# Sparse attention scores on TensorE: the low-part product widened from 64 to 128 stationary rows

## The chip, the cores and the metric

The kernel runs on one core of a Trainium2 chip. The metric is the device time of one execution in microseconds (us). Three executions of the kernel before took 1151.09, 1152.84 and 1153.11 us; the median is 1152.84 us.

## What is computed

Two layers over 256 tokens of 1024 features. Each layer is half a SwiGLU block, a token mixer, and half a SwiGLU block, each followed by a residual, a layer norm and a modulation. The mixer of layer 0 is retention, that of layer 1 sparse attention with 16 heads in 4 groups. With 256 tokens all four key blocks are selected and the window holds all keys, so two of its three branches are dense causal attentions over 256 keys, each with keys and values of its own:

```python
q = q.reshape(B, S, G, HPG, dh) * (dh ** -0.5)          # G 4, HPG 4, dh 64
s = jnp.einsum('qghd,gqnkd->ghqnk', qi, k_g) - slopes * dist_s      # branch "selected"
...
s = jnp.einsum('qghd,kgd->ghqk', qi, kwb) - slopes * dist_w         # branch "window"
p = masked_softmax(s, mask_w, -1)
...
o = gb[..., 0:1] * o_cmp + gb[..., 1:2] * o_sel + gb[..., 2:3] * o_win
```

The change touches the two einsums for `s`: a product of queries and keys over dh = 64.

## The kernel before

Every fp32 value that enters a product is split exactly into a high and a low float32r part, and a product is the sum of high by high, high by low and low by high. Weights stream in as chunks of [128, 2048] (1 MB), are split into `wh` and `wl` by ScalarE, VectorE and GpSimd, and are used by TensorE in the order of a written plan.

Sparse attention is stage 4 of 6. Its work is a hand-written list of step names, `NSA_STEPS`, which `Program.run` calls one after the other; each step issues its instructions on its engine at once, so the list fixes the order on every engine. The steps of interest:

- `feat.nk.n`, `feat.nq.g`: 24 products for each 128 features of keys (two groups and both branches) or queries, into one PSUM bank (lines L520 to L522).
- `keyshi`, `keyslo`, `keystwice` (`keys_parts`): keys of two groups as [dh, group, branch, key]. Tile `k1` has 128 partitions and holds the high parts twice, in partitions 0 to 63 and 64 to 127. Tile `k2` has 64 partitions and holds the low parts.
- `qhi`, `qlo` (L1322, L1327): tile `qs` per group, with a head's high part in partitions 0 to 63 and its low part in 64 to 127.
- `score.g.hd` (`do_score`, L1339 to L1342), 16 times: one head's scores for both halves of the queries. For the first 128 queries, 256 columns (128 keys of two branches) in bank `px`: `qs` with all 128 rows against `k1` (high by high plus low by high), and then rows 0 to 63 of `qs` against `k2` (high by low), added in the same bank. For the other 128 queries the same with 512 columns in bank `py`. The queries are the stationary operand, so each of the four instructions has a weight load of its own.
- `dist.g.hd.t` (L1358): VectorE adds the distances to a bank's scores and takes the minima; this frees the bank. `px` and `py` come from a pool of four banks, so a head's banks are those of two heads earlier. `exp` (L1369) on ScalarE follows.
- `turn`, `turnhi`, `turnlo`, `mix`: probabilities transposed (L1461), split, and multiplied with the values (L1490).
- `enter` (`Sparse.enter`), a step of the list that leads from stage 3 to stage 4: allocates the tiles of the stage and zeroes some of them on GpSimd (L1097, L1098, L1101), then the low part of the gates' weights (L1108). GpSimd next computes the norm's `lnr` (L334).

A score in the list's order is `do_score`:

```python
T.matmul(x[:, :SEQ], q[0], k1[:, :, :P], start=True, stop=False)
T.matmul(x[:, :SEQ], q[0][:64], k2[:, :, :P], start=False, stop=True)
```

Of the kernel before, what the change touches and what calls it, by code (L numbers as in the profile page):

```python
# [17 lines left out]
P = 128  # L18
D = 1024
KT = D // P  # L20
SEQ = 256
# [25 lines left out]
def outs_due(first, i, done):  # L47
    """Whether the second product's chunk follows the first product's chunk i"""
    if done == NF // 2 - TAIL or 2 * done + 3 > i:
        return False  # L50
    return not first or done < i - NHEAD + 1


# The model's first products, feature block by feature block as the modulation comes, for groups of 4 column blocks:
# for the first NSOON feature blocks k the groups 0 and 1, then group 2; for the others the groups 1 and 2, then group 0.
# ("in0", [(k, group), (k, group)])
# [8 lines left out]
def stream_plan():  # L65
    """Weight chunks [128, 2048] in the order in which they are used."""
# [214 lines left out]
def tile_model(ctx, tc, io):  # L281
# [49 lines left out]
    def rstd_of(var, eps, name, by=1.0):  # L331
        """(by * var + eps) ** -0.5, [128, 1]"""
        r = work.tile([P, 1], F32, name=name, tag="rstd", bufs=4)
        G.tensor_scalar(r, var, by, eps, op0=ALU.mult, op1=ALU.add)  # L334
        G.tensor_tensor(r, r, mhalf, op=ALU.pow)
        return r

# [28 lines left out]
    # what is emitted with the chunks: modulation units at an even rate, and work put off by some chunks  # L366
# [19 lines left out]
    def to_row(s):  # L386
        """cols[s, 2] as a row of features, in DRAM"""
# [9 lines left out]
    def shift_scale(s):  # L397
        """A part's input is xn * cols[s, 0] + cols[s, 1]."""
# [10 lines left out]
    def gate(s):  # L409
        """cols[s, 2] = residual weight * (1 + gate)"""  # L410
# [27 lines left out]
    def prefetch(upto, vcols=VCOLS, acols=CH, lag=False, late=None):  # L438
        """The high parts of the first acols by ScalarE, the others' by GpSimd; the low parts of the first vcols by
        VectorE, with lag not before the next chunk's; late: which columns are put off, and by which engines"""  # L440
# [25 lines left out]
    def get(key, n=SEQ, ahead=AHEAD, vcols=VCOLS, far=FAR_AHEAD, acols=CH, lag=False):  # L466
        """A chunk's parts as [128, k, n]."""
# [9 lines left out]
    # Work in an order given by names of steps: what a step does, its arguments, and the engine where another is meant  # L477
    # than the usual one.
    class Program:
# [12 lines left out]
        # chunks: "fetch", "hi" by column range, "lo" by column range  # L492
# [22 lines left out]
    def b_side(ps, w, off, n, hT):  # L515
        """ps[n, 256] = w[:, k, off:off+n].T @ h.T"""
# [7 lines left out]
    def a_side(ps, w, ks, t, hT):  # L524
        """ps[128 tokens, n] += h[t] @ w, for the blocks ks of the features"""
# [7 lines left out]
    def first_part(part, key, n, j, t, i, q, x, total=4):  # L533
        """The same in parts, in any order: q: half of the features; x = 0: their high parts, x = 1: their low parts"""
# [13 lines left out]
    def out_side(y, t, half, w, j, f, first, last):  # L548
        """y[half] += f[t] @ w[j], for the piece's columns"""
# [27 lines left out]
    class Parts:  # L577
        """The second product's left side by blocks of 128 features, two to a tile."""
# [14 lines left out]
    def banks_y(s):  # L593
        """For each half of the tokens pieces of the columns; at the end of the model the last ones are shorter"""
# [6 lines left out]
    def outs(ys, parts, w, i):  # L601
        """All tokens, blocks i and i + 1"""
# [5 lines left out]
    def tail(part, t, g):  # L608
        """The last blocks, for one half of the tokens, in three or four parts"""
# [15 lines left out]
    kept = {}  # L625

    class Norm:
# [39 lines left out]
        def half(self, t, h, ys):  # L667
            """The same at the end of the model, with the statistics by pieces"""
# [15 lines left out]
        def last(self, t):  # L684
# [3 lines left out]
            def affine(e, cs):  # L688
                """The rest on VectorE, or all of it on ScalarE and GpSimd"""
# [23 lines left out]
        # the next part's input, features on partitions  # L713
# [23 lines left out]
        # the part's output, for the next residual  # L737
# [20 lines left out]
    class Ffn:  # L758
# [11 lines left out]
        def act(self, i, ps):  # L770
            """gate | up in one bank, features on partitions"""
# [9 lines left out]
        # the first products, one half of the tokens at a time  # L781
# [61 lines left out]
    class Start(Program):  # L843
# [43 lines left out]
        def do_first(self, k, p, g):  # L887
            """p: high by high, high by low, low by high parts; g: group of columns"""
# [15 lines left out]
        # the first group's first feature blocks wait on chip, to be added later  # L904
# [35 lines left out]
    class Retention:  # L940
# [14 lines left out]
        # the first products, one half of the tokens at a time  # L955
# [38 lines left out]
        def scores(self, h, q, k):  # L994
            """[keys, queries] with the decay: keys 0 to 127 by all queries, the other keys by the later half"""
# [83 lines left out]
    class Sparse(Program):  # L1079
# [7 lines left out]
        def enter(self, ctx, hT):  # L1087
# [3 lines left out]
            for name, shape in (("dist", [P, 2, P]), ("slope", [P, NH]), ("cdist", [P, 2, 16]),  # L1091
                                ("cmask", [P, 2, 16]), ("pe", [P, 2, 16]), ("w2", [P, 2, 2, DH])):
                self.c[name] = pool.tile(shape, F32, name=name)
                nc.sync.dma_start(self.c[name], io[name])
            self.kc12 = pool.tile([P, NG, 2, 16], F32R, name="kc12")
# [14 lines left out]
        # the first products, one half of the tokens at a time  # L1110
# [22 lines left out]
        # The steps between the values' products and the second product's tail.  # L1133
# [10 lines left out]
        # 256 features on partitions, by 128  # L1144
# [5 lines left out]
        # gates: high and low parts of the weights side by side; their products are added with the tokens on partitions  # L1150
# [33 lines left out]
        # the blocks to be compressed: [(l % 2, dh), l // 2, (group, block)]  # L1184
# [29 lines left out]
        # first layer, then the activation with the features on partitions: x / (1 + exp(-2 u))  # L1214
# [42 lines left out]
        # compressed keys: high parts and low parts, each twice over the partitions  # L1257
# [15 lines left out]
        # compressed values: high, high and low parts over the partitions, for two heads  # L1273
# [26 lines left out]
        # keys: [dh, group, branch, key]: high parts, twice over the partitions, and low parts  # L1300
        def keys_parts(self, n, br):
            if n not in self.k:
                self.k[n] = [self.pool.tile([n, 2, 2, SEQ], F32R, name=f"k{x}", tag=f"k{x}") for x, n in ((1, P), (2, 64))]
# [13 lines left out]
        # queries over the negated slopes; high part over low part  # L1317
# [14 lines left out]
        # a head's negated scores, then with the distances, and their minima; e: [head, branch, key] for the first half of  # L1332
        # the queries, then for the second half two heads to a tile
        def do_score(self, g, hd):
            k1, k2 = [x[:n, g % 2] for n, x in zip((P, 64), self.k[g // 2])]
# [4 lines left out]
            T.matmul(x[:, :SEQ], q[0][:64], k2[:, :, :P], start=False, stop=True)  # L1340
            T.matmul(y, q[1], k1.rearrange("p b n -> p (b n)"), start=True, stop=False)
            T.matmul(y, q[1][:64], k2.rearrange("p b n -> p (b n)"), start=False, stop=True)  # L1342
# [21 lines left out]
        # probabilities, times the gates  # L1364
# [26 lines left out]
        # compressed keys  # L1391
# [44 lines left out]
        def do_chi(self, g, e=G):  # L1436
            """High, low and high parts side by side"""
            copy(e, self.e3[:, :, 0], self.ec[g][0].rearrange("p a b c -> p (a b) c"))
# [8 lines left out]
        # probabilities with the keys on partitions, by the values; n: the branches' halves of the keys, last the compressed  # L1447
# [250 lines left out]
```

## Time and profile before

| | us |
|---|---|
| median of 3 runs (1151.09 to 1153.11) | 1152.84 |
| span of the profiled execution, first to last instruction | 1149.6 |
| PE busy | 1116.2 (97%) |
| DVE busy | 901.8 (78%) |
| ACT busy | 555.3 (48%) |
| POOL busy | 153.2 (13%) |

The profile gives the span of the profiled execution; of the time around it only the difference to the runs is known, 3.2 us to the median. Mean granted clock of TensorE over the span is 0.988. Stage 4 lies between about 797 and 940 us. A busy PE is not a PE at its peak: the ends of matmuls are modelled, and what a matmul costs in a stream is the distance from its start to the next start.

### The profile page before, as it was taken

The numbers are of one execution on the slowest core, as the hardware profiler recorded it, in microseconds if no ns is written. First come the engines' busy times: TensorE is split into PE (matmuls) and PEld (weight loads), VectorE is DVE, ScalarE is ACT, GpSimd is POOL, SyncE is SP. The second block draws the span as 40 slices with busy tenths as digits, with TensorE's granted clock in tenths as the row PEclk, the third lists the DMA queues.
The fourth block names the chain that finished last, engine by engine and source line by source line (L and its number), as shares of the span: only waits on it lengthen the run. The fifth ranks groups of instructions, "written<-read, shape, count | busy, mean of one in ns | idle before, by whom it ended". The sixth has DMA issues, their size and how long they took to land.

```text
span 1149.6 us, 18937 instructions
## 1 busy us (share of the span) xinstructions
PE 1116.2 (97%) x7444; PEld 1023.2 (89%) x7444; DVE 901.8 (78%) x1535; ACT 555.3 (48%) x955; POOL 153.2 (13%) x219
## 2 busy tenths in 40 slices
PE   6999999999999999999999999999899999999996
PEld 6999988898988899999999999988778679999995
DVE  7989886778788878997587987767987987765555
ACT  3555344444344553444464444456676865444341
POOL 0030000011010300000000000022366731000003
PEclk9999999999999999999999999999988999999998
DMA  9978986657877468997548988756631254665550
GB/s 325 369 259 339 352 305 236 242 196 290 335 301 269 163 243 316 383 370 300 202 145 332 356 301 315 273 184 220 196 135 38 74 202 178 244 230 210 202 201 37
DMA packets 55912, 283.50 MB, mean 247 GB/s; under 512 B 7008, under 2 KB 9104, under 8 KB 34064
## 3 DMA queue, kind: packets, MB, share of 16 engines
q1 hardware_dynamic: 55536, 282.19, 66.3%
q8 instruction: 58, 0.95, 0.3%
q14 instruction: 30, 0.25, 0.1%
q10 hardware_dynamic: 288, 0.11, 0.0%
HBM read 280.15 MB, written 2.12 MB: 246 GB/s over the span
## 4 chain that ended last, share of the span: by engine, by line
PE 86%; DVE 9%; issue 2%; DMA 2%; ACT 1%; POOL 0%; SPq 0%; POOLq 0%; DVEq 0%; ACTq 0%
PE pb L520 11%; PE pb L522 11%; PE pb L521 11%; PE y L555 8%; PE y L554 8%; PE y L553 8%; PE pf L545 6%; PE p L901 6%; DVE wl L512 3%; PE prg L529 1%; PE prg L531 1%; PE prv L529 1%; PE prv L530 1%; PE prg L530 1%; PE prv L531 1%
## 5 line engine op out<-in xcount | busy, mean ns | idle before, releaser
L453 DVE TENSOR_TENSOR wl<-raw,wh 128x1024 fp32r<-128x1024 f32 x252 | 299.7, 1233 | 34.7 <-ACT wh L448 34.1
L520 PE MATMUL pb<-hh,wh 128*128 128x256 f32 x1072 | 303.9, 283 | 0.0
L522 PE MATMUL pb<-hh,wl 128*128 128x256 f32 x1072 | 303.3, 283 | 0.0
L521 PE MATMUL pb<-hl,wh 128*128 128x256 f32 x1072 | 303.3, 283 | 0.0
L448 ACT ACTIVATE wh<-raw 128x1024 fp32r<-128x1024 f32 x252 | 248.3, 1049 | 11.1 <-DMA raw<-in_w 9.2
L520 PEld LDWEIGHTS pb<-hh,wh 128*128 128x128 f32 x1072 | 205.6, 192 | 1.3
L521 PEld LDWEIGHTS pb<-hl,wh 128*128 128x128 f32 x1072 | 205.7, 192 | 0.9
L522 PEld LDWEIGHTS pb<-hh,wl 128*128 128x128 f32 x1072 | 205.6, 192 | 0.0
L359 DVE SCALAR_TENSOR_TENSOR ada_w<-ada_w,cb 128x1024 f32<-128x1024 f32 x144 | 173.9, 1228 | 6.6 <-DMA ada_w<-in_ada_w 6.4
L553 PE MATMUL y<-wh,fh 128*128 128x512 f32 (+2 forms) x462 | 176.5, 382 | 0.0
L555 PE MATMUL y<-wh,fl 128*128 128x512 f32 (+2 forms) x462 | 175.4, 380 | 1.1 <-DVE fl L559 1.1
L554 PE MATMUL y<-wl,fh 128*128 128x512 f32 (+2 forms) x462 | 175.8, 380 | 0.0
L773 ACT ACTIVATE sa<-pb 128x256 f32<-128x256 f32 x67 | 25.7, 383 | 291.3 <-PE pb L522 288.3
L512 DVE TENSOR_TENSOR wl<-raw,wh 128x512 fp32r<-128x512 f32 x190 | 134.2, 750 | 3.8 <-ACT wh L571 2.8
L774 DVE TENSOR_TENSOR sa<-sa,pb 128x256 f32<-128x256 f32 x67 | 28.1, 419 | 105.1 <-ACT sa L773 105.1
L571 ACT ACTIVATE wh<-raw 128x1024 fp32r<-128x1024 f32 x93 | 94.1, 1050 | 21.0 <-DMA raw<-in_w 19.7
L555 PEld LDWEIGHTS y<-wh,fl 128*128 128x128 f32 x462 | 86.8, 188 | 17.3 <-DVE fl L559 1.5
L553 PEld LDWEIGHTS y<-wh,fh 128*128 128x128 f32 x462 | 86.9, 188 | 14.5
L554 PEld LDWEIGHTS y<-wl,fh 128*128 128x128 f32 x462 | 86.9, 188 | 14.4 <-DVE wl L453 0.2
L575 POOL TENSOR_SCALAR wh<-raw 128x1024 fp32r<-128x1024 f32 x11 | 13.7, 1245 | 326.5 <-DMA raw<-in_w 316.0
L512 POOL TENSOR_TENSOR wl<-raw,wh 128x512 fp32r<-128x512 f32 x34 | 50.3, 1491 | 45.6 <-ACT wh L571 26.5
L545 PE MATMUL pf<-wh,hh 128*128 128x256 f32 (+1 forms) x200 | 56.1, 310 | 0.0
(318 smaller groups left out, 1778.6 us busy)
## 6 DMA issues: line engine op xcount, KB each, us to landing
raw<-in_w SPq DMA_DIRECT2D x170, 1024.0 KB, 5.2
ada_w<-in_ada_w SPq DMA_DIRECT2D x144, 512.0 KB, 6.8
raw<-in_w SPq DMA_DIRECT2D x24, 512.0 KB, 7.7
ln<-in_ln_rows SPq DMA_DIRECT2D x12, 512.0 KB, 7.7
g<-r_dram SPq DMA_DIRECT2D x6, 512.0 KB, 6.2
xT<-in_xT SPq DMA_DIRECT2D x8, 128.0 KB, 5.1
x<-in_x SPq DMA_DIRECT2D x2, 512.0 KB, 8.2
x_dram<-u SPq DMA_DIRECT2D x2, 512.0 KB, 6.9
```

The lines of the kernel that those rows point to most:

```text
L359: V.scalar_tensor_tensor(w, w, 1.0, cb, op0=ALU.mult, op1=ALU.mult, accum_out=mod[:, l, u:u + 1])
L448: A.activation(hi[:, a:a + HI], raw[:, a:a + HI], AF.Copy)
L453: e.tensor_tensor(lo[:, a:b], raw[:, a:b], hi[:, a:b].bitcast(F32), op=ALU.subtract)
L512: e.tensor_tensor(lo[:, a:b], raw[:, a:b], hi[:, a:b].bitcast(F32), op=ALU.subtract)
L520: T.matmul(ps, a, hh[:, k, :], start=k == 0, stop=False)
L521: T.matmul(ps, a, hl[:, k, :], start=False, stop=False)
L522: T.matmul(ps, b, hh[:, k, :], start=False, stop=k == KT - 1)
L545: T.matmul(ps[:, :n], s, part.w[i][y][:, first + k], start=(done, k, y) == (1, 0, 0), stop=(done, k, y) == (total, 3, 1 - x), skip_group_c ...
L553: T.matmul(y, sh, hi[:, j, cs], start=first, stop=False)
L554: T.matmul(y, sh, lo[:, j, cs], start=False, stop=False)
L555: T.matmul(y, sl, hi[:, j, cs], start=False, stop=last)
L571: A.activation(o, i, AF.Copy)
```

## The change

Tile `k2` gets 128 partitions. It is allocated once, when the stage is entered, and GpSimd writes zeros into its partitions 64 to 127 (64 x 1024 elements) there. The low parts of the keys are written to partitions 0 to 63 as before, for both pairs of groups in the same tile. The second product of each score takes all 128 rows of `qs` as its stationary tile and all 128 partitions of `k2` as the moving one, so rows 64 to 127 meet zeros. The number of instructions on PE, their order and their columns are the same, and each keeps its own weight load. Comments and docstrings, which the change also drops, are left out of this diff.

```diff
@@ Sparse.enter
+            self.k2 = pool.tile([P, 2, 2, SEQ], F32R, name="k2")
+            G.tensor_scalar(self.k2[64:].rearrange("p g b n -> p (g b n)").rearrange("p (a b) -> p a b", b=P),
+                            ident[64:, None, :].to_broadcast([64, 8, P]), 0.0, 0.0, op0=ALU.mult, op1=ALU.add)
             self.kc12 = pool.tile([P, NG, 2, 16], F32R, name="kc12")
@@ keys_parts
-                self.k[n] = [self.pool.tile([n, 2, 2, SEQ], F32R, name=f"k{x}", tag=f"k{x}") for x, n in ((1, P), (2, 64))]
+                self.k[n] = [self.pool.tile([P, 2, 2, SEQ], F32R, name="k1", tag="k1"), self.k2]
@@ do_score
-            k1, k2 = [x[:n, g % 2] for n, x in zip((P, 64), self.k[g // 2])]
+            k1, k2 = [x[:, g % 2] for x in self.k[g // 2]]
...
-            T.matmul(x[:, :SEQ], q[0][:64], k2[:, :, :P], start=False, stop=True)
+            T.matmul(x[:, :SEQ], q[0], k2[:, :, :P], start=False, stop=True)
...
-            T.matmul(y, q[1][:64], k2.rearrange("p b n -> p (b n)"), start=False, stop=True)
+            T.matmul(y, q[1], k2.rearrange("p b n -> p (b n)"), start=False, stop=True)
```

The one place where the order of an engine changes is GpSimd at `enter` (names with their buffer numbers; `k` is `k2`). Before:

```order
L335 TENSOR_TENSOR lnr<-lnr,mhalf 128x1 [waits Pool_49]
L1097 TENSOR_SCALAR e_7903<-ident 128x8x16 [waits DMAHW4_49,DVE_49,PE_49]
L1098 TENSOR_SCALAR kc_7902<-ident 128x128 [waits PE_49]
L1101 TENSOR_SCALAR vc<-ident 112x128 x4
L1108 TENSOR_TENSOR ghl<-gw,ghl 128x8x48 [waits DMAHW5_49,Activation_49]
L334 TENSOR_SCALAR lnr<-sm 128x1 [waits Activation_49]
```

With the change:

```order
L335 TENSOR_TENSOR lnr<-lnr,mhalf 128x1 [waits Pool_49]
L1097 TENSOR_SCALAR k_7902<-ident 64x1024 [waits DVE_49,DMAHW4_49,PE_49,Pool_49]
L1101 TENSOR_SCALAR e_7905<-ident 128x8x16 [waits Pool_49]
L1102 TENSOR_SCALAR kc_7904<-ident 128x128
L1105 TENSOR_SCALAR vc<-ident 112x128 x4
L1112 TENSOR_TENSOR ghl<-gw,ghl 128x8x48 [waits DMAHW5_49,Activation_49]
L334 TENSOR_SCALAR lnr<-sm 128x1 [waits Activation_49]
```

One instruction more stands ahead of the other zeroings, which move by its length. It takes over the waits that the first of them had, and one on GpSimd itself.

## Rows read from the trace of the kernel before

**Rows 1.** The page, part 1: busy time of each engine, its share of the span, and its instructions.

```profile
PE 1116.2 (97%) x7444; PEld 1023.2 (89%) x7444; DVE 901.8 (78%) x1535; ACT 555.3 (48%) x955; POOL 153.2 (13%) x219
```

**Rows 2.** Busy time by stretch, over the part of stage 4 in which the scores lie: us, busy us and instructions of PE, PEld, DVE, ACT and POOL, then TensorE's granted clock as a share of 2.4 GHz, the DMA share and GB/s.

```profile
800.00:860.00 60.00, 54.10 (x348) 46.07 (x347) 54.55 (x134) 42.23 (x105) 28.77 (x27) 0.91 0.47 159
860.00:912.00 52.00, 48.73 (x280) 38.97 (x280) 42.88 (x142) 38.69 (x125) 38.11 (x77) 0.90 0.12 41
```

**Rows 3.** Timeline of PE: score 1.2 at full clock with the instruction behind it, and the first instructions of scores 1.0 and 1.1, at half clock. Columns: start us, us, engine, line, operation, out<-in, stationary rows*columns, moving partitions x columns, count, idle before and its releaser.

```profile
855.63 0.36 PE L1339 MATMUL px<-k,qs 128*128 128x256 f32 x1
855.93 0.38 PE L1340 MATMUL px<-k,qs 64*128 64x256 f32 x1
856.24 0.49 PE L1341 MATMUL py<-k,qs 128*128 128x512 f32 x1
856.66 0.50 PE L1342 MATMUL py<-k,qs 64*128 64x512 f32 x1
857.09 1.96 PE L1396 MATMUL pxc<-kc,qs 128*128 128x32 f32 x16
...
840.98 0.38 PE L1339 MATMUL px<-k,qs 128*128 128x256 f32 x1 [2.66 <-DVE qs L1327]
...
843.25 0.58 PE L1339 MATMUL px<-k,qs 128*128 128x256 f32 x1
```

**Rows 4.** Timeline of PE in the change from stage 3 to stage 4: products of a 128-row tile of `hh` with `wh` and then with `wl`, where both instructions load the same stationary tile; 256 columns, then 512.

```profile
786.36 0.28 PE L545 MATMUL pf<-wl,hh 128*128 128x256 f32 x1
786.48 0.29 PE L545 MATMUL pf<-wh,hh 128*128 128x256 f32 x1
...
787.19 0.40 PE L545 MATMUL pf<-wh,hh 128*128 128x512 f32 x1
787.43 0.40 PE L545 MATMUL pf<-wl,hh 128*128 128x512 f32 x1
```

**Rows 5.** Timeline of the weight loads (PEld) in a stream of 128-row products with 256 columns, at full clock.

```profile
829.10 0.19 PEld L520 LDWEIGHTS pnq<-hh,wh 128*128 128x128 f32 x1
829.22 0.19 PEld L521 LDWEIGHTS pnq<-hl,wh 128*128 128x128 f32 x1
```

**Rows 6.** Timeline of PE at half clock: two products of 128 rows and 256 columns in a stream.

```profile
821.03 0.42 PE L1223 MATMUL ph<-wl,b 128*60 128x256 f32 x1
821.24 0.42 PE L1221 MATMUL ph<-wh,b 128*120 128x256 f32 x1
```

**Rows 7.** Timelines of PE and VectorE (DVE), scores of group 0: waits.

```profile
827.12 0.36 PE L1339 MATMUL px<-k,qs 128*128 128x256 f32 x1 [0.20 <-DVE nmax L1358]
...
835.08 0.69 DVE L512 TENSOR_TENSOR wl<-raw,wh 128x512 fp32r<-128x512 f32 x1 [0.26 <-PE pnq L522]
```

**Rows 8.** Timeline of DVE, scores of group 1: its waits for PE.

```profile
845.82 0.48 DVE L1358 CUSTOM_DVE_ANT_0 e<-py,dist,slope 128x256 f32<-128x256 f32 x1 [1.57 <-PE py L1342]
849.18 3.16 DVE L512 TENSOR_TENSOR wl<-raw,wh 128x512 fp32r<-128x512 f32 x2 [0.37 <-PE ph L1223]
855.98 0.28 DVE L1237 COPY hT<-pht 128x120 f32<-128x120 f32 x1 [0.90 <-PE pht L1232]
857.20 0.48 DVE L1358 CUSTOM_DVE_ANT_0 e<-py,dist,slope 128x256 f32<-128x256 f32 x1 [0.54 <-PE py L1342]
```

**Rows 9.** Timelines of DVE and ScalarE (ACT), scores of group 2: their waits for PE.

```profile
879.09 0.69 DVE L1471 TENSOR_TENSOR pTl<-ppt,pTh 128x512 fp32r<-128x512 f32 x1 [0.42 <-PE pno L1490]
882.75 0.35 DVE L1358 CUSTOM_DVE_ANT_0 e<-px,dist,slope 128x128 f32<-128x128 f32 x1 [2.11 <-PE px L1340]
889.89 0.69 DVE L573 CAST pTh<-ppt 128x512 fp32r<-128x512 f32 x1 [3.89 <-PE ppt L1461]
...
889.46 1.55 ACT L1322 ACTIVATE qs<-pnq 64x256 fp32r<-64x256 f32 x4 [4.54 <-PE pnq L522]
```

**Rows 10.** Timeline of DVE, scores of group 3 and after: its waits for PE.

```profile
896.94 0.48 DVE L1358 CUSTOM_DVE_ANT_0 e<-py,dist,slope 128x256 f32<-128x256 f32 x1 [0.22 <-PE py L1342]
899.53 0.35 DVE L1358 CUSTOM_DVE_ANT_0 e<-px,dist,slope 128x128 f32<-128x128 f32 x1 [0.45 <-PE px L1340]
902.49 0.48 DVE L1358 CUSTOM_DVE_ANT_0 e<-py,dist,slope 128x256 f32<-128x256 f32 x1 [0.24 <-PE py L1342]
913.53 0.69 DVE L573 CAST pTh<-ppt 128x512 fp32r<-128x512 f32 x1 [0.34 <-PE ppt L1461]
```

**Rows 11.** Busy time by stretch, columns as in rows 2.

```profile
842.00:848.00 6.00, 6.00 (x17) 3.80 (x18) 4.09 (x20) 3.52 (x11) 4.93 (x5) 0.50 0.23 96
879.00:889.00 10.00, 10.00 (x43) 8.68 (x43) 4.79 (x19) 2.02 (x8) 3.93 (x9) 0.50 0.00 1
904.00:908.00 4.00, 2.34 (x11) 1.35 (x10) 3.91 (x11) 3.98 (x14) 4.00 (x10) 1.00 0.05 20
```

**Rows 12.** Timelines of GpSimd (POOL) at `enter`, and of one DVE instruction beside it.

```profile
763.49 0.61 POOL L1097 TENSOR_SCALAR e<-ident 128x128 fp32r<-128x128 f32 x1 [170.64 <-issue]
...
764.76 2.82 POOL L1101 TENSOR_SCALAR vc<-ident 112x128 fp32r<-112x128 f32 x4
767.55 1.01 POOL L1108 TENSOR_TENSOR ghl<-gw,ghl 128x384 fp32r<-128x384 f32 x1
773.93 0.19 POOL L334 TENSOR_SCALAR lnr<-sm 128x1 f32<-128x1 f32 x1 [5.37 <-ACT u L662]
...
767.34 1.77 DVE L512 TENSOR_TENSOR wl<-raw,wh 128x512 fp32r<-128x512 f32 x1
```

## The prediction, made before the changed kernel was run

> **What bounds the kernel now.** I read the page first: PE is busy for 97% of the span [rows 1], so what is taken from PE's path may shorten the run, if it is taken where PE is what the others wait for. The share is an average, so the second view is busy time by stretch, over the part in which the changed instructions lie [rows 2]: from 800 to 912 us PE is busy for 102.8 of 112 us, DVE for 97.4, ACT for 80.9. Here two engines are nearly full, and PE's granted clock is 0.91 and 0.90, not 1. So a microsecond that PE saves is worth one only where DVE or ACT stood waiting for PE, and the third view must be the timelines, engine by engine, for the rows with an idle time before them and who ended it.
>
> **What a score costs on PE, and why.** A score is four instructions. At full clock their starts lie 0.30, 0.31, 0.42 and 0.43 us apart, together 1.46 us up to the next instruction [rows 3]. The same columns cost far less elsewhere: 256 columns against a 128-row tile take 0.12 us from start to start and 512 take 0.24, also where two instructions in a row load the same stationary tile, as the changed score will [rows 4]. In such a stream each weight load lasts 0.19 us yet starts 0.12 us after the one before [rows 5], so loads run beside products. The score's distances exceed the stream's by about 0.19 each (0.31 against 0.12, 0.43 against 0.24), which is one load's length: between its instructions nothing overlaps. What sets these four apart from the stream is that their stationary tiles alternate between 128 and 64 rows [rows 3]. I take that alternation as the cause. Without it a score should cost 0.12 + 0.12 + 0.24 + 0.24 = 0.72 us: a saving of 0.74.
>
> Three scores (1.0, 1.1 and 2.3) run at half clock, 1.2 GHz. The first takes 843.25 - 840.98 = 2.27 us [rows 3]; 256 columns in a stream take 0.21 there [rows 6], so 512 are estimated at 0.42 and the changed score at 1.26: a saving of 1.0. In all PE saves 13 x 0.74 + 3 x 1.0 = 12.6 us. That is the most that the edit can give unless the clock itself changes.
>
> **How much of it reaches the end.** By places, each bounded by what PE frees and by the waiting for PE that is there to be removed:
>
> - *Scores of group 0 (818 to 836 us).* PE itself waits for DVE here, 0.20 us before score 0.2 for DVE to free a bank; a shorter score waits longer. DVE waits for PE once, 0.26 us [rows 7]. Gain 0.3 of 3.0 saved.
> - *Group 1 (841 to 857).* PE frees 2 x 1.0 + 2 x 0.74 = 3.5 us; DVE waits for PE for 1.57 + 0.37 + 0.90 + 0.54 = 3.4 us [rows 8]. If the clock comes back at the same moment, near 848 us, the 2.0 us freed at half clock are filled with work that would have taken 1.0 at full clock, so 2.5 is left. Bounds 2.5 and 3.4; I take 2.5, the clock as it is recorded.
> - *Group 2 (873 to 889).* PE frees 3 x 0.74 + 1.0 = 3.2 us. DVE waits 0.42 + 2.11 + 3.89 = 6.4 us and ACT 4.54 for the last queries [rows 9], so cover is not short and the saving is PE's own. Score 2.2 comes two heads after 2.0 and needs its banks, which DVE frees no earlier; I take 0.4 off. Gain 2.8.
> - *Group 3 (895 to 909).* PE frees 4 x 0.74 = 3.0 us, but DVE waits only 0.22 + 0.45 + 0.24, and 0.34 after them [rows 10]. Beyond that DVE is the bound: gain 1.2, and PE then waits for DVE. Between groups, and from 914 to 940 us, no score is left to gain from; the stages behind start earlier by what was gained.
>
> Sum: 0.3 + 2.5 + 2.8 + 1.2 = 6.8 us.
>
> **The zeroing.** GpSimd gets one instruction of 64 x 1024 at `enter`. The trace has no such shape. The nearest rows there are 128 columns in 0.61, and four of 128 in 2.82 [rows 12]; from one to eight of those lengths makes 0.6 to 5.6 us. Queued behind it on GpSimd are the other zeroings and `ghl`, needed tens of us later, and then `lnr`, on which the norm's path hangs; before `lnr` GpSimd idles 5.37 us [rows 12]. So on its own path it costs 0 to 0.3, and I take 0. It also runs beside DVE: one `wl` took 1.77 us beside `ghl` where 0.69 is its usual length [rows 7, 12], so a slowdown is possible, 0 to 1.1; `ghl` reads two tensors and the zeroing one, and I take 0.2. No wait is added on PE, since `k2`'s zeros are written some 50 us before the first score, and no transfer is added or moved.
>
> Net gain 6.6 us: 1152.84 - 6.6 = **1146.2 us**. The durations are from one execution with a span of 1149.6 us, 3.2 below the median of the runs; the gain is taken off the median, as time around the span should not change.
>
> **A rule that speaks against it.** The trace shows 128-row loads starting while products of other 128-row tiles run [rows 5]. The Trainium skill, "TensorE: Matmul & The Clock Gate", section on the mechanism of packing small matmuls, states that a weight load overlaps with matmuls in flight only when their row groups differ. By that rule a score of four full-height tiles would still pay four loads behind its products and cost about what it does now, and the time would be that of the first rival. These rows do not agree with it as it stands, which is why that rival has a small chance.
>
> **Rivals.**
>
> 1. *Height is not the cause, nothing is saved.* For it: a distance that is longer by one load is what any failing overlap would give, and the trace has no other 64-row tile. Against: the same stationary tile twice in a row, float32r and 512 columns are all present in rows 4, without the extra. Then only the zeroing is left: 1153.0 us. Chance 0.08.
> 2. *DVE takes it all.* PE saves, but in groups 1 and 3 DVE's own queue, with ACT and GpSimd behind it, was about as late as PE, and only the full-clock scores of group 2 pay less the bank wait: 3 x 0.74 - 0.4 = 1.8 us, so 1151.0. For it: DVE's 97.4 busy us [rows 2]. Against: 3.89 and 1.57 us in one piece waiting for PE [rows 8, 9]. Chance 0.05.
> 3. *The clock helps.* The clock is at half from 842 to 848 and from 879 to 889 us, with PE never idle in these rows [rows 11], part of the time in scores whose products are spread out. With dense scores it may rise sooner or not fall. Ten us at half clock hold five us of work at full clock; one us of the five is counted above, so up to 4 more, and 0.9 in group 1: 1141.3 us. Chance 0.21.
> 4. *The clock hurts: slower.* Shorter scores leave PE waiting more in group 3, where it already idles 1.66 of 4 us at full clock [rows 11]; an idle of 2.66 us stands before score 1.0, which is the first at half clock [rows 3, 11]. A fall there lasting as long as the one from 879 to 889 us costs half of 10 us, 5, where PE binds; net gain 1.6. It decides from 13 us of low clock, where the gain is gone, and from 18 us the run is slower by over 0.2%; with the clock low from 895 to 920 us: 1152.84 - 6.6 + 12.5 = 1158.7 at most. Against: the idle of 904 to 908 does not trip it now [rows 11]. Chance 0.05.
>
> **How the numbers follow.** The forecast has 0.61. No change means within 0.2% (2.3 us), about what runs of this kernel can tell. Forecast and rival 3 are faster: 0.82. Rivals 1 and 2 are the same: 0.13. Rival 4: 0.05. The low end is the whole saving of 12.6 us, which also takes in rival 3: 1140.0. The high end is 3 x 0.74 = 2.2 us gained, the full-clock scores of group 2 alone, rounded: 1150.5. That leaves out rivals 1, 2 and 4, 0.18.
>
> **What would show it.** In the timeline after: distances of 0.12 and 0.24 inside a score, about 0.72 from its first start to the next instruction, loads starting 0.12 apart. DVE's waits of 1.57, 2.11 and 3.89 us should shrink, and new waits of PE for DVE appear around score 0.2 and in group 3. GpSimd's `lnr` should keep an idle time before it. The prediction is wrong if a score still takes 1.4 us, if score 3.3 starts less than 3 us earlier although scores are short, or if the granted clock falls where it did not before.

## The result, and the profile after

The changed kernel takes 1142.2 us (median of 4 runs, 1141.25 to 1143.25), the kernel before 1152.97 us beside it (4 runs, 1151.09 to 1154.38). The ratio is 0.9909 [0.9893, 0.9925], a gain of 10.8 us with an interval of 8.7 to 12.3. The forecast was 6.6, so the direction and the range held and the size was too small. The profiled execution has a span of 1139.6 us (its own time 1141.55), 10.0 us less than before. The reading below finds these 10.0 us in the trace.

First the page, busy time by engine, after; it answers to [rows 1]:

```profile
PE 1101.2 (97%) x7444; PEld 1017.3 (89%) x7444; DVE 901.4 (79%) x1535; ACT 555.7 (49%) x955; POOL 153.4 (13%) x220
```

PE has lost 15 us of busy time with the same 7444 instructions, and its share has stayed at 97%, since the span shrank with it. The other engines have the work that they had, and GpSimd has one instruction more.

Is it the scores? This is PE's timeline of score 1.2 with the instruction behind it, in the columns of [rows 3], which it answers to:

```profile
852.85 0.37 PE L1343 MATMUL px<-k,qs 128*128 128x256 f32 x1
853.05 0.29 PE L1344 MATMUL px<-k,qs 128*128 128x256 f32 x1
853.17 0.40 PE L1345 MATMUL py<-k,qs 128*128 128x512 f32 x1
853.41 0.39 PE L1346 MATMUL py<-k,qs 128*128 128x512 f32 x1
853.64 1.85 PE L1400 MATMUL pxc<-kc,qs 128*128 128x32 f32 x16
```

From the first start to the next instruction it takes 853.64 - 852.85 = 0.79 us, where it took 1.46. The distances inside are 0.12, 0.24 and 0.23, those of the 128-row stream [rows 4]; only the first is 0.20, behind an instruction of another kind. The timeline of the weight loads of the same score says why:

```profile
852.93 0.19 PEld L1344 LDWEIGHTS px<-k,qs 128*128 128x128 f32 x1
853.05 0.19 PEld L1345 LDWEIGHTS py<-k,qs 128*128 128x128 f32 x1
853.17 0.19 PEld L1346 LDWEIGHTS py<-k,qs 128*128 128x128 f32 x1
```

Loads that last 0.19 start 0.12 apart, each while a product runs, as in [rows 5]. Now busy time by stretch after, with the columns of [rows 2]; the first two rows answer to those, the third to the first of [rows 11], and the last two lie around the scores of groups 2 and 3:

```profile
800.00:860.00 60.00, 51.68 (x386) 48.77 (x386) 57.26 (x142) 45.94 (x115) 31.80 (x32) 0.94 0.49 165
860.00:912.00 52.00, 46.15 (x305) 38.60 (x303) 49.60 (x148) 43.27 (x136) 42.81 (x88) 0.97 0.19 63
842.00:848.00 6.00, 6.00 (x41) 5.70 (x41) 5.88 (x20) 5.00 (x18) 5.76 (x6) 0.80 0.18 76
870.00:890.00 20.00, 18.67 (x131) 15.57 (x130) 19.63 (x74) 17.95 (x61) 15.79 (x29) 1.00 0.01 2
896.00:900.00 4.00, 4.00 (x20) 3.45 (x19) 3.00 (x11) 1.73 (x7) 2.41 (x6) 0.62 0.00 0
```

Two things are to be seen. VectorE has become the fuller engine: 106.9 of 112 us, and PE 97.8 (before 97.4 and 102.8). And the granted clock has changed: from 870 to 890 us it is 1.00, and the same stretch before reads

```profile
870.00:890.00 20.00, 18.98 (x90) 15.11 (x90) 12.80 (x52) 10.43 (x32) 12.32 (x24) 0.74 0.01 2
```

with ten microseconds of it at 1.2 GHz [rows 11]. In group 1 the clock is at full speed again from about 844 us, where it had been 848. A short fall is new, at 896 to 900 us (0.62).

The waits that were to shrink are gone. Between 840 and 900 us VectorE's timeline shows one wait, where [rows 8, 9] had up to 3.89 us in one piece. PE waits for VectorE instead. This is what the timelines of VectorE and of PE print with an idle time before it: VectorE's one wait, and some of PE's:

```profile
897.15 0.69 DVE L573 CAST pTh<-ppt 128x512 fp32r<-128x512 f32 x1 [0.61 <-PE ppt L1465]
```

```profile
827.91 0.47 PE L1345 MATMUL py<-k,qs 128*128 128x512 f32 x1 [0.33 <-DVE nmax L1362]
...
840.59 0.39 PE L1343 MATMUL px<-k,qs 128*128 128x256 f32 x1 [3.43 <-DVE qs L1331]
...
895.58 0.69 PE L1494 MATMUL pno<-pTl,vals 128*64 128x512 f32 x1 [1.99 <-DVE pTl L1475]
```

Last the zeroing: timelines of GpSimd and VectorE at `enter` after, which answer to [rows 12], and of the PE instruction that waits there.

```profile
763.38 1.27 POOL L1097 TENSOR_SCALAR k<-ident 64x1024 fp32r<-64x1024 f32 x1 [170.73 <-DVE fl L559]
...
774.93 0.19 POOL L334 TENSOR_SCALAR lnr<-sm 128x1 f32<-128x1 f32 x1 [5.98 <-ACT u L662]
...
763.66 7.05 DVE L512 TENSOR_TENSOR wl<-raw,wh 128x512 fp32r<-128x512 f32 x7
...
769.56 0.50 PE L554 MATMUL y<-wl,fh 128*128 128x512 f32 x1 [1.20 <-DVE wl L512]
```

The zeroing itself takes 1.27 us and `lnr` keeps its idle time. But the seven splits on VectorE beside it take 7.05 us, where the same seven took 5.85 before, and PE waits 1.20 us for one of them.

Where the 10.0 us come from, by the starts of the same instructions in the two traces:

| up to | before | after | gained | forecast |
|---|---|---|---|---|
| score 0.0 (entry, with the zeroing) | 818.34 | 819.41 | -1.07 | -0.2 |
| score 1.0 (group 0) | 840.98 | 840.59 | +1.46 | +0.3 |
| `pxc` behind score 1.2 (group 1) | 857.09 | 853.64 | +3.06 | +2.5 |
| score 2.0 (between) | 872.95 | 869.59 | -0.09 | 0 |
| score 3.0 (group 2 and what follows it) | 895.45 | 885.50 | +6.59 | +2.8 |
| score 3.3 (group 3) | 907.03 | 896.77 | +0.31 | +1.2 |
| end of the span | 1149.6 | 1139.6 | -0.26 | 0 |

### The profile page after: what moved, and what is told of

The parts are those of the page before. It is cut to its first block, busy times and chain, and to the rows that moved or that the text cites. A ratio compares the mean times of both kernels' runs of the same rounds, so it can differ in the third digit from the quotient of the medians.

```text
span 1139.6 us, 18939 instructions
## 1 busy us (share of the span) xinstructions
PE 1101.2 (97%) x7444; PEld 1017.3 (89%) x7444; DVE 901.4 (79%) x1535; ACT 555.7 (49%) x955; POOL 153.4 (13%) x220
## 4 chain that ended last, share of the span: by engine, by line
PE 85%; DVE 10%; issue 2%; ACT 1%; DMA 1%; POOL 0%; SPq 0%; POOLq 0%; DVEq 0%; ACTq 0%
PE pb L520 11%; PE pb L522 11%; PE pb L521 11%; PE y L554 8%; PE y L555 8%; PE y L553 8%; PE pf L545 7%; PE p L901 6%; DVE wl L512 3%; DVE e L1362 1%; PE prg L529 1%; PE prg L531 1%; PE prv L530 1%; PE prv L531 1%; PE prv L529 1%
## 5 line engine op out<-in xcount | busy, mean ns | idle before, releaser
L512 DVE TENSOR_TENSOR wl<-raw,wh 128x512 fp32r<-128x512 f32 x190 | 131.5, 735 | 4.3 <-ACT wh L571 4.0
L554 PEld LDWEIGHTS y<-wl,fh 128*128 128x128 f32 x462 | 86.9, 188 | 15.9 <-DVE wl L512 1.6
```

The costliest lines, as they stand in the source:

```text
L512: e.tensor_tensor(lo[:, a:b], raw[:, a:b], hi[:, a:b].bitcast(F32), op=ALU.subtract)
L554: T.matmul(y, sh, lo[:, j, cs], start=False, stop=False)
```

## The experiments

Each was timed beside the kernel before. Ratios are to the kernel before, with 95% intervals. A gain in us is the difference of the two medians; a range of gains is worked out from the interval.

**The zeroing alone.** The changed kernel with its second products back on 64 rows:

```
- T.matmul(x[:, :SEQ], q[0], k2[:, :, :P], start=False, stop=True)
+ T.matmul(x[:, :SEQ], q[0][:64], k2[:64, :, :P], start=False, stop=True)
  (and the same for y)
```

> The changed kernel with the second products put back to 64 rows, so that only the 128-partition tile and its zeroing on GpSimd are left. Theory A, that the seven low-part splits of VectorE beside the zeroing are slowed by it (they took 7.05 us against 5.85): 0.9 to 1.3 us slower than before, the splits again near 7.0 us, scores of 1.46 us. Rival, that the zeroing is hidden and the late start of the first score is chance: within 0.3 us of before.

1153.84 us, ratio 1.0002 [0.9989, 1.0016]: without the height there is no gain, within an interval from 1.3 us faster to 1.8 slower (0.9 to 1.3 slower was expected). The profile shows the splits slowed as in the changed kernel, and the clock of group 2 as in the kernel before:

```profile
870.00:890.00 20.00, 20.00 (x100) 15.54 (x99) 14.22 (x53) 11.90 (x34) 13.77 (x25) 0.73 0.01 2
...
763.95 7.01 DVE L512 TENSOR_TENSOR wl<-raw,wh 128x512 fp32r<-128x512 f32 x7
```

What one zeroing costs the run is below the resolution of this comparison; further down it is read from the traces.

**The zeroing four times.** The changed kernel with the instruction in a loop:

```
+ for _ in range(4):
      G.tensor_scalar(self.k2[64:]..., 0.0, 0.0, op0=ALU.mult, op1=ALU.add)
```

> The changed kernel with the zeroing at entry issued four times, 5.1 us of GpSimd in place of 1.3. Theory A, each zeroing slows VectorE's splits beside it by 0.9 to 1.2 us and the chain carries it: 2.5 to 3.6 us slower than the changed kernel, if lnr behind it on GpSimd is still in time. Rival, VectorE is slowed but the later wait for a transfer at about 798 us takes it up: within 0.5 us of the changed kernel.

1143.91 us, ratio 0.992 [0.9907, 0.9933]; the changed kernel beside it took 1141.39 (0.9901 [0.9886, 0.9916]). So three more zeroings cost 2.5 us, 0.84 each (by means 2.2 ± 1.5), although `lnr` still waits for ScalarE behind them. Its timelines of GpSimd and VectorE:

```profile
763.59 5.62 POOL L1098 TENSOR_SCALAR k<-ident 64x1024 fp32r<-64x1024 f32 x4 [170.72 <-DVE fl L559]
...
763.87 8.75 DVE L512 TENSOR_TENSOR wl<-raw,wh 128x512 fp32r<-128x512 f32 x7
```

VectorE's splits go from 7.05 to 8.75 us while GpSimd works beside them. That is 1.70 of the 2.5 us; the rest is within the noise.

**The zeroing later.** It is taken out of `enter` and becomes a step of its own, behind the first splits of `nq`:

```
- fetch.ck.0 hi.nq.0.0.1024@G lo.nq.0.0.512@G lo.nq.0.512.1024@G post.0.0.0@V ...
+ fetch.ck.0 hi.nq.0.0.1024@G lo.nq.0.0.512@G lo.nq.0.512.1024@G keyszero post.0.0.0@V ...
```

> The changed kernel with the zeroing moved from the entry of the stage to a point about 33 us later, after GpSimd's low parts of the first query weights, where GpSimd idles 5.6 us and VectorE waits for a transfer. Theory A: 1.0 us faster than the changed kernel (1141.2), the splits at 5.9 us and the first score about 1.0 us earlier. Rival, zeroing costs nothing: 1142.2, no difference. Against both: if group 0 absorbs a later start in its waits for VectorE, less than 0.5 us is gained.

It took 1139.98 us (0.9882 [0.9861, 0.9903]). It was run again with the changed kernel beside it:

> The changed kernel with the zeroing about 33 us later, now beside the changed kernel itself. Theory A, a zeroing at entry costs what three more of them cost, about 0.84 us each by the run with four: 0.8 to 1.2 us faster than the changed kernel. Rival, the stages behind take it up: within 0.3 us of it.

> The changed kernel, for comparison with the next three on the same chip: 10.5 to 12.5 us under the kernel before.

1139.82 us (0.9906 [0.9889, 0.9924]) against 1142.24 (0.9924 [0.9908, 0.9941]): 2.4 us better than the changed kernel, where about one was expected, and the fastest of all versions. Over all runs the medians are 1139.99 (10 runs) and 1142.05 (16 runs), and the means differ by 2.1 ± 1.1. Timelines of GpSimd and VectorE in the first of its two profiles:

```profile
593.80 2.58 POOL L1103 TENSOR_SCALAR vc<-ident 112x128 fp32r<-112x128 f32 x4
767.13 1.03 POOL L1110 TENSOR_TENSOR ghl<-gw,ghl 128x384 fp32r<-128x384 f32 x1 [170.75 <-ACT ghl L1108]
...
796.19 1.05 POOL L1310 TENSOR_SCALAR k<-ident 64x1024 fp32r<-64x1024 f32 x1
...
764.19 5.13 DVE L512 TENSOR_TENSOR wl<-raw,wh 128x512 fp32r<-128x512 f32 x7
```

The edit did more than it was meant to. In the changed kernel `k2`'s zeroing is the one that waits until 763 us for its memory, and the others queue behind it; with it out of the way they run 170 us earlier. There they stand beside other splits of VectorE, which they lengthen a little (one takes 0.78 us and the next two 1.47, in the changed kernel 0.68 and 1.28). The seven splits at `enter` now take 5.13 us, 1.92 less than in the changed kernel and 0.72 less than before, and score 0.0 starts at 818.18 and 818.25 us in the two profiles, where the changed kernel has 819.41. That is 1.2 us of the gain. About one more lies around score 3.3, where the granted clock differs. Busy time by stretch around score 3.3, first in the changed kernel, then with the late zeroing:

```profile
895.00:905.00 10.00, 9.42 (x51) 7.90 (x52) 8.53 (x24) 7.14 (x24) 8.17 (x20) 0.83 0.00 2
```

```profile
895.00:905.00 10.00, 7.99 (x53) 6.44 (x51) 9.87 (x29) 8.83 (x32) 8.84 (x24) 1.00 0.07 30
```

From the start of score 3.3 to the end of the span both profiles of the late zeroing take 241.8 us, and the six profiles with the zeroing at `enter` and no 64-row product in the scores take 242.8 to 243.3: in those six the clock falls in this stretch (0.83 in each), in these two it doesn't. Why a zeroing in another place goes with that was not tested, and the parts were not run apart.

**Group 2 alone, and all but group 2.** The changed kernel with 128 rows in some groups and 64 in the others:

```
+ rows = P if g in (2,) else 64          # the other run: g in (0, 1, 3)
- T.matmul(x[:, :SEQ], q[0], k2[:, :, :P], start=False, stop=True)
+ T.matmul(x[:, :SEQ], q[0][:rows], k2[:rows, :, :P], start=False, stop=True)
  (and the same for y)
```

> The changed kernel with 128 rows for the four scores of group 2 only; the other twelve second products have 64 rows. Theory B, that most of the extra gain is the clock that no longer falls to half at the scores of group 2: 4.5 to 6 us faster than before (6.6 in that stretch, less 1.1 for the zeroing), the granted clock at full from 870 to 886 us. Rival, that the gain follows the time freed on TensorE, score by score: 4 of 16 scores, about 2 us after the zeroing, and the fall stays.

> The changed kernel with group 2 left at 64 rows; groups 0, 1 and 3 have 128. Theory B, that group 2 and the clock there carry most: 3 to 5 us faster than before, the granted clock at half again for about 10 us around score 2.3, whose four instructions then take 2.4 us. Rival, gain by freed time: 12 of 16 scores, 8 us. With the group-2-only run at 7 us faster, the two should add up to the whole change, 10.7, plus the zeroing counted twice, about 1.

Group 2 alone: 1146.68 us, 0.9938 [0.9922, 0.9954], 6.9 us faster than the kernel before beside it. All but group 2: 1150.63 us, 0.9971 [0.9959, 0.9983], 3.2 us faster. Together 10.1, though both pay for the zeroing, so one group of four carries two thirds, and the table of places above is borne out by runs. Busy time by stretch, first with group 2 alone, then all but it:

```profile
870.00:890.00 20.00, 18.93 (x144) 16.90 (x144) 19.60 (x63) 17.30 (x52) 16.60 (x32) 1.00 0.01 2
```

```profile
870.00:890.00 20.00, 19.43 (x88) 15.04 (x88) 12.76 (x51) 10.53 (x36) 10.91 (x22) 0.74 0.01 2
```

The fall of the clock stays where the scores of group 2 alternate, and goes where they don't, whatever the other groups do.

**Two changes of height in place of four.** The kernel before with two lines swapped; no zeroing, no wider tile:

```
  T.matmul(x[:, :SEQ], q[0], k1[:, :, :P], start=True, stop=False)
- T.matmul(x[:, :SEQ], q[0][:64], k2[:, :, :P], start=False, stop=True)
  T.matmul(y, q[1], k1.rearrange("p b n -> p (b n)"), start=True, stop=False)
+ T.matmul(x[:, :SEQ], q[0][:64], k2[:, :, :P], start=False, stop=True)
  T.matmul(y, q[1][:64], k2.rearrange("p b n -> p (b n)"), start=False, stop=True)
```

> The kernel before, all second products with 64 rows, but a score's four instructions in the order px with k1, py with k1, px with k2, py with k2: the height of the stationary tile changes twice a score and not four times. Theory H, each change of height costs about 0.19 us: a full-clock score takes 1.10 us from its first start to the next instruction, and the run is 3 to 5 us faster than before. Rival L, a load is exposed wherever it or the one before has 64 rows: three exposed loads, 1.29 us a score, 1.5 to 3 us faster. Rival S, only the length of the columns counts and the order nothing: 1.46 us, no change.

1144.65 us (six runs, 1143.97 to 1145.66 but for one of 1151.88), ratio 0.9935 [0.991, 0.9961]: 9.0 us by medians, 4.5 to 10.4 by the interval, where 3 to 5 was expected. PE's timeline of score 2.1, which stands right behind score 2.0, then its weight loads on 64 rows, and the stretch:

```profile
871.73 0.39 PE L1339 MATMUL px<-k,qs 128*128 128x256 f32 x1
871.95 0.39 PE L1340 MATMUL py<-k,qs 128*128 128x512 f32 x1
872.27 0.38 PE L1341 MATMUL px<-k,qs 64*128 64x256 f32 x1
872.49 0.38 PE L1342 MATMUL py<-k,qs 64*128 64x512 f32 x1
872.81 1.06 PE L1396 MATMUL pxc<-kc,qs 128*128 128x32 f32 x8
...
872.27 0.18 PEld L1341 LDWEIGHTS px<-k,qs 64*128 64x128 f32 x1 [0.25 <-issue]
872.38 0.19 PEld L1342 LDWEIGHTS py<-k,qs 64*128 64x128 f32 x1
```

```profile
870.00:890.00 20.00, 19.15 (x126) 15.13 (x127) 18.73 (x69) 16.11 (x55) 15.29 (x30) 1.00 0.01 2
```

A score takes 872.81 - 871.73 = 1.08 us, with 1.10 expected: 0.72 and twice 0.18, where the kernel before has 0.72 and four times 0.19 (1.48 for its own score 2.1, from 874.40 to 875.88). The cost of a change does not lie at the change alone. The distances are 0.22, 0.32, 0.22 and 0.32, each 0.08 to 0.10 longer than in the stream: a change lengthens the distance that ends in it, and the next one. Two 64-row products in a row (0.22) stand as two of 128 rows do behind a change (0.22), and the second one's load starts while the first one runs, so it is the change that costs, not the small tile.

The granted clock stays at 1.00 from 870 to 890 us here too, which goes with so large a gain from half of the changes. The long run has the lowest mean clock of the six, 0.987 where the others have 0.988 to 0.991; where its clock fell is not recorded.

**Heights of 96 rows.** The changed kernel with `q[0][:96]`, `k2[:96]`, and the same for `y`:

> The changed kernel with 96 rows in the second products in place of 128. Theory P, it is the half-height tile that cannot follow a full one: 96 rows run like 128, 0.72 us a score, and the time of the changed kernel within 0.5 us. Rival Q, any two unequal heights in a row expose the load: 1.46 us a score and 1152 to 1154 us, the time of the kernel before plus the zeroing.

1142.51 us, 0.9924 [0.9908, 0.994], as the changed kernel beside it (1142.24). PE's timeline:

```profile
871.21 0.28 PE L1343 MATMUL px<-k,qs 128*128 128x256 f32 x1
871.33 0.28 PE L1344 MATMUL px<-k,qs 96*128 96x256 f32 x1
871.45 0.39 PE L1345 MATMUL py<-k,qs 128*128 128x512 f32 x1
871.68 0.40 PE L1346 MATMUL py<-k,qs 96*128 96x512 f32 x1
871.92 0.96 PE L1400 MATMUL pxc<-kc,qs 128*128 128x32 f32 x8
```

0.71 us, though the heights alternate. Unequal heights alone cost nothing; 64 beside 128 does. The Trainium skill, "TensorEngine Tiling (Array Packing)", section on key properties of the tiling modes, says that changing the mode, not the tile alone, drains TensorE, and it lists modes of 128, 64 and 32 rows and none of 96. These traces agree in that the change costs and 96 rows go with 128; the price here is 0.18 to 0.19 us for a change. Whether it is a drain or a load that is no longer hidden, they do not tell apart.

**Why does the clock not fall in group 2?** Less work on PE, or time freed for the other engines, could have done it as well as the missing stalls. The first run leaves the second products of group 2 out of the kernel before:

```
- T.matmul(x[:, :SEQ], q[0], k1[:, :, :P], start=True, stop=False)
- T.matmul(x[:, :SEQ], q[0][:64], k2[:, :, :P], start=False, stop=True)
+ T.matmul(x[:, :SEQ], q[0], k1[:, :, :P], start=True, stop=g == 2)
+ if g != 2:
+     T.matmul(x[:, :SEQ], q[0][:64], k2[:, :, :P], start=False, stop=True)
  (and the same for y)
```

> The kernel before, but group 2's scores without the high-by-low products (the part left out): two instructions of 128 rows a score, no zeroing. This frees more of TensorE's time than the change does there, 1.46 - 0.36 = 1.1 us a score against 0.74, and takes the work itself away. Theory F, freed time and the end of the exposed loads are what count: the clock stays at full and the run is 7 to 9 us faster than before. Theory D, TensorE's clock holds only while it is filled with work: with less to do in that stretch the clock falls to half there as before, and the run is only 3 to 5 us faster.

1145.29 us, 0.9933 [0.9917, 0.9949]. Busy time by stretch:

```profile
870.00:890.00 20.00, 18.21 (x139) 16.09 (x137) 19.59 (x61) 16.74 (x50) 17.12 (x31) 1.00 0.01 2
```

No fall, so half the products with no alternation keep the clock as well as all of them with none. The second run issues the second products of group 2 three times in the changed kernel, all with 128 rows, so that a score takes about as long as before:

```
- T.matmul(x[:, :SEQ], q[0], k2[:, :, :P], start=False, stop=True)
+ for n in range(3 if g == 2 else 1):
+     T.matmul(x[:, :SEQ], q[0], k2[:, :, :P], start=False, stop=n == 2 or g != 2)
  (and the same for y)
```

> The changed kernel, but group 2's second products are issued three times each, all of 128 rows (the high-by-low part is counted three times): 0.12 x 4 + 0.24 x 4 = 1.44 us a score, as long as before the change, without a change of height. Theory X, the exposed loads are what goes with the fall of the clock: clock at full from 870 to 890 us, and 2 to 3.5 us slower than the changed kernel (4 x 0.72 us of added work on a path that is TensorE's). Theory Y, TensorE's freed time is what keeps the clock: the clock falls to half there again, and the run is 6 to 9 us slower than the changed kernel.

1142.89 us, 0.9925 [0.991, 0.9941], 0.65 us over the changed kernel beside it (by means 0.1 ± 1.4), where 2 to 3.5 was expected. PE's timeline with the first product of score 2.0, score 2.1, and the first product of score 3.0, then the stretch:

```profile
869.63 0.37 PE L1343 MATMUL px<-k,qs 128*128 128x256 f32 x1
...
871.12 0.28 PE L1343 MATMUL px<-k,qs 128*128 128x256 f32 x1
871.24 0.52 PE L1345 MATMUL px<-k,qs 128*128 128x256 f32 x3
871.60 0.40 PE L1346 MATMUL py<-k,qs 128*128 128x512 f32 x1
871.83 0.86 PE L1348 MATMUL py<-k,qs 128*128 128x512 f32 x3
872.53 0.96 PE L1402 MATMUL pxc<-kc,qs 128*128 128x32 f32 x8
...
886.92 0.28 PE L1343 MATMUL px<-k,qs 128*128 128x256 f32 x1
```

```profile
870.00:890.00 20.00, 19.75 (x141) 17.55 (x141) 17.68 (x68) 16.21 (x56) 14.53 (x29) 1.00 0.01 2
```

The score takes 872.53 - 871.12 = 1.41 us, almost as long as before, and yet the clock does not fall. So neither the shorter score nor the time that it frees keeps the clock; what is left that differs from the kernel before is the alternation of heights.

The trace also parts the gain of group 2. From score 2.0 to score 3.0 this kernel takes 886.92 - 869.63 = 17.29 us, the changed kernel 15.91, the kernel before 22.50. The added 2.8 us of products (four scores with 0.7 more) lengthen the group by 1.38; the other half falls into time in which PE waited. The remaining 22.50 - 17.29 = 5.2 us go, by this estimate, with the clock. Other profiles bear this out: wherever group 2 has 128 rows and one product of each kind the same stretch takes 15.8 to 15.9 us, in the three with four changes of height 22.5 to 23.9, and with two changes 16.5.

**The changed kernel again.** It was run beside three of these:

> The changed kernel as it is, beside the three below on one chip: 1142.2 us as before, 10 to 11 us under the kernel before; mean granted clock 0.992 to 0.994 against 0.985 to 0.988. If the clock in the stretch of group 2 decides, runs of this kernel with a lower mean clock are the longer ones.

1141.39 us, as given with the zeroing four times: 12.5 under the kernel before, where 10 to 11 was expected. The last sentence of what was expected is not borne out: its six runs do not get longer with a lower mean clock (1143.13 us at 0.995, 1141.07 at 0.992). In the later repeat, beside the late zeroing, the changed kernel took 1142.24 us, and its gain of 9.1 falls short of the 10.5 to 12.5 expected, since the kernel before took 1151.37 beside it, where it had 1152.97 to 1153.87.

## Why the prediction was right, and where it was off

**The cost of a score: right.** 0.72 us was forecast, 0.70 to 0.81 is shown at full clock where no wait lies in the score (score 2.1: 871.09 - 870.39 = 0.70), and at half clock score 1.1 takes 843.03 - 841.75 = 1.28, with 1.26 forecast. That the alternation is the cause is shown from three sides: by the change, by two changes in place of four (1.08), and by 96 rows (0.71).

**Rivals 1 and 2: wrong.** The zeroing alone gives 1153.84 us and 64-row tiles keep their stalls. The rule of the Trainium skill, "TensorE: Matmul & The Clock Gate", section on the mechanism of packing, that a load overlaps with products in flight only where the row groups differ, is not what these traces show: loads of full height start 0.12 us apart beside full-height products. VectorE did become the fuller engine, but only after PE had given the group its 6.6 us.

**The step that failed: "group 2, gain 2.8".** It measured 6.59. The term was made from the rows as they stood: three scores at full clock, one at half, less 0.4 for a bank, and nothing for the clock, which was left falling from 879 to 889 us. The clock did not fall. The ten microseconds at 1.2 GHz held five of work at 2.4 GHz, as rival 3 had it. By the estimate from the run with the second products three times, 5.2 of the 6.59 us go with the clock and only 1.4 with the shorter scores, so the term was too large for the scores and left out the larger part. With it VectorE's 6.4 us of waiting for PE and ScalarE's 4.54 [rows 9] went. The forecast's size was thus off by a mechanism that stood among the rivals with 0.21 and gave 1141.3, near the measured 1142.2. What could have spoken for it was in the rows: PE's row has no idle time from 879 to 889 us [rows 11], so an idle engine was no explanation for the low clock there. Runs show which of these matters: group 2 on 128 rows alone brings the full clock and 6.9 us, the rest without it leaves 0.74 and brings 3.2.

As a cross-check, the low clock in all: the mean granted clock of the span is about 0.985 before and 0.993 after. A microsecond at half clock counts for a half in that mean, so this is 2 x 0.015 x 1150 = 34 us at 1.2 GHz against 2 x 0.007 x 1140 = 16. Among 45 runs of the kernel before, the time rises by about a third of a us for each us of low clock, so 18 us less are an estimated 6 us; the rest of the gain is the shorter scores themselves.

**The smaller terms.** Group 1 gave 3.06, forecast 2.5 with bounds to 3.4: the clock came back at 844 us instead of 848. (Rows 8 and 9 leave out two waits of VectorE for PE, 0.24 us at 843.35 and 0.47 at 875.13, which move neither term.) Group 3 gave 0.31, forecast 1.2: VectorE was the bound even more than assumed, and PE then waits 1.99 us for it at 895.58, with the clock low from 896 to 900. That is rival 4's mechanism, and one of the things that the prediction said would make it wrong: the clock fell where it had not before. It was short, and it is not the wait alone: in the two profiles of the late zeroing a wait of 2.02 and 2.03 us stands at the same place and the clock does not fall. The errors of the terms other than group 2 nearly cancel in this execution (-0.87 at the entry, +1.16 in group 0, +0.56 in group 1, -0.89 in group 3, -0.35 between and behind), and that is luck.

**The zeroing: mis-sized.** 0.2 was taken, with bounds 0 to 1.1; the entry lost 1.07. The price came by the path that was named, VectorE beside GpSimd, but as a delay of seven splits and not of one. Other profiles agree on the size: score 0.0 starts at 818.31 to 819.09 us in the three without a zeroing of `k2`, and at 819.13 to 820.53 in the eight with one at `enter`, 1.2 later in the mean. In this execution group 0 makes it up, with 1.46 instead of 0.3, and not by its scores: five splits that VectorE has ahead of the first distances take 5.28 us, where they took 6.37 before, since GpSimd's own splits beside them start later (825.60 us, before 824.31). In the profile of the repeated run the five take 6.39 again. So the 1.46 is in part an accident of one execution, and the cost of the zeroing is read across runs: about 1.2 us at the entry, and 0.84 us for each further one. The 2.1 us that the later place brings hold more than that, a fall of the clock in group 3 that does not come.

**Open.** Why the clock falls with the exposed loads of group 2 is not settled: four changes of height in a score go with a fall in that group in every profile (before, the zeroing alone, all but group 2), two changes or none go with none. Neither the amount of work nor the time freed explains it. Nor is the fall certain: single runs that have no profile show a mean clock of 0.991, such as 1148.01 us of the kernel before (mostly 0.985) and 1145.35 us of all but group 2 (0.984 to 0.988), and may have gone without it. Groups 1 and 3 have falls of their own that were not taken apart; in group 3 four changes of height go without one before, and no change goes with one after.

## What to carry to other kernels

Tiles of 64 rows that alternate with full-height ones in a stream cost about a load's length each time the height changes; put products of equal height together, which needs no memory, or pad the short tile with zeros (96 rows do as well). Zero such padding where VectorE is not reading two tensors beside it, and look at which instruction of the queue holds the others back. Before a saving on the busiest engine is priced, read the granted clock of the stretch: a stretch at half clock with the engine never idle may be worth more than its stalls, and where it comes back the next engine, here VectorE, sets the end.

## What the runs showed of the hardware

- A change between a stationary tile of 128 rows and one of 64 costs 0.18 to 0.19 us, as long as a load, spread over the distance that ends in it and the next; a change between 128 and 96 rows costs nothing (0.71 us for four products).
- The clock can stand at 1.2 GHz through ten microseconds in which PE's row shows no idle time, and stay at 2.4 with the same products and 128-row tiles (0.74 against 1.00 over 870 to 890 us).
- A GpSimd instruction with one input, 64 x 1024, slows the subtracts on VectorE beside it: seven splits take 5.13 us with only `ghl` beside them, 5.85 with the small zeroings too, 7.05 with the large one as well, 8.75 with four large ones. The Trainium skill, "GPSIMD Engine Reference", section Specifications, says that GpSimd shares its SBUF interfaces with VectorE, with contention where an instruction of VectorE has two SBUF inputs. A split reads `raw` and `wh`, and these rows agree.
